# First output product of a two-layer encoder: two block products in other PSUM banks, a residual behind its difference, a scaling ahead of two casts

## The chip, the cores and the metric

The kernel runs on one core of a Trainium2 chip, as one launch. Its five engines are named as in the profile: PE (TensorE, matrix products; PEld is its loading of weights), DVE (VectorE), ACT (ScalarE), POOL (GpSimd) and SP (SyncE, which here only sends transfers; POOL and ACT send some too). Each engine works through its own list in order and waits on semaphores that the others raise. Matrix products write to PSUM, eight banks of 128 x 512 floats. The metric is the time of an execution in microseconds (us), smaller is better.

## The reference, cut to what matters

The input `x` is 512 x 1024 in float32, and there are two layers. `proj` of a layer goes into its token mixer (dilated window attention in layer 0, grouped-query attention in layer 1), into the queries of an attention over 256 memory tokens, and into a gate. The results are gated and go through one output projection, whose product is added to `x`.

```python
for i in range(DEPTH):                       # 2 layers
    h = rmsnorm(x, norm_g[i])
    proj = jnp.einsum('bsd,de->bse', h, w_in_a[j])      # w_in_b in layer 1
    o_mix = mixer_dilated(qkv, ...)          # 8 heads; mixer_axial_gqa in layer 1
    o_mem = memory_attention(q_mem, mem_h, ...)         # 4 heads
    y = jnp.concatenate([o_mix, o_mem], axis=-1) * jax.nn.silu(gate)
    x = x + jnp.einsum('bse,ed->bsd', y, w_out[i])
```

The change lies around the last line of layer 0, "the first output product": `y` is 512 x 1536, `w_out` is 1536 x 1024. The result is both the residual of layer 1 and, normed, the operand of layer 1's projection. Ahead of it stands the end of the eighth window head, where the unnormalized probabilities `p` of its dilations are scaled by softmax weights and added up.

## The kernel before, in words

**Products.** Each float32 product is made in three passes on numbers with fewer bits: high part by high part (line L177), high part by low part of the operand (L178), and low part of the weights by high part of the operand (L181). Weights come from DRAM in pieces of 128 x 1024 (`wl`); ACT casts the high part `wh` (L321), DVE subtracts it for the low part `wo` (L331). One piece serves one step of 12 matmuls: 8 with `wh` (4 on L177, 4 on L178) and 4 with `wo`.

**Seven products for eight.** A chunk is cut into quarters, and `s_chunk` makes it with seven block products in place of eight, from sums of quarters of the operand and of the weights. In the first output product their order is 11, S3, 12, S1, S2, S4, 22 (`PRODUCTS_3`); S2 goes on in the banks of S3, S4 in those of S1. Each has three steps. A product fills two PSUM banks (`bank[s]`, two units of 128 rows), which `s_chunk` takes from the pool `pj` of four banks (`fresh` products only). The other four banks are the pool `at`, from which the attention takes scores, transposes (`pt`, `xT`) and outputs (`oo`). The operand sums are `yS` and their low parts.

**After a product.** A table (`after`) says what follows: `hold` copies the banks to SBUF on ACT (L429: 11, S3 and S1); `add_11` copies 12's banks on ACT (L438) and adds them by DMA (L440); `fold`, after S2, makes on DVE the quarter "21" (`t3`, L447), the quarter "12" and the difference `t5 - t3` (L450), where `t5` is the copy of S1, later the quarter "22"; two `add` at the end finish "12" and "21" on DVE (L422) out of S4 and 22. The difference "22" needs nothing more. The tiles of the four quarters are the halves of the rows' accumulators `acc`.

**The residual.** `ahead` (in `out_proj`) brings `x` in: for quarter "12" by a plain load from SP (L1103), for "21" and "22" by a DMA from POOL that adds into the tile (L1105), for "11" by one too (L1094). The one for "22" is sent right behind the copy of S1 in `hold`, so that DVE's difference (L450) is made out of a tile into which a transfer writes, and waits for it. The one for "21" is sent behind the difference, which reads `t3`.

**Behind it.** When both halves of a block of rows are done, `ev_o` stores them (L1590), takes the sum of squares and norms them on DVE into `m` (L567), PE transposes `m` (`xT`, L573), and the next projection begins (`act`).

**The order.** Nothing is scheduled by a planner: the order of all engines is that in which the program writes the instructions. A `Driver` counts slots, one a step of a product. `release` and `spawn` give it generators that go on when their slot has come, `soon` puts a function at the very start of the next slot, `late` at its end. The eighth head (`attn_a` with `h == 7`) is such a generator; its `scale(1)`, `scale(0)` (L1507 on ACT for this head, four pieces each), `turn` (transposes, L1523, and their copies, L1527) and `pv` (`oo`) are apart by the slots of `Y`. In the slot of `scale(0)` ACT also has a cast of `yS` (L932) and a tanh of the gate (L899).

Of the kernel before, what the change touches and what calls it, by code (L numbers as in the profile page):

```python
# [132 lines left out]
def trunk_kernel(ctx: ExitStack, tc: tile.TileContext, x, mem, wall, norm_g, mem_norm_g, gcol,  # L133
# [9 lines left out]
    drv = Driver()  # L143
# [10 lines left out]
    def pj(name="pj"):  # L154
        return psum.tile([128, 512], F32, tag="pj", name=name, bufs=4)

    def at(name="at"):
        return psum.tile([128, 512], F32, tag="at", name=name, bufs=4)
# [16 lines left out]
    def mm_early(o, a, b, c, d, start):  # L175

        T.matmul(o, a, b, start=start, stop=False, skip_group_check=True)  # L177
        T.matmul(o, c, d, start=False, stop=False, skip_group_check=True)  # L178

    def mm_late(o, a, b, stop):  # L180
        T.matmul(o, a, b, start=False, stop=stop, skip_group_check=True)  # L181
# [208 lines left out]
    def s_chunk(n, act, ev, tokens=True, pre=None, half=False, soon=False, tight=False, place=None, pairs=False, K=4, tail=None, turn=None, late=None, ahead=None):  # L390


        units, per = n // 256, 1024 // n
        bank, snap = [None, None], {}
# [32 lines left out]
        def hold(name, u, b):  # L427
            t = snap[name, u] = place({"z": "11", "s3": "21", "s5": "22"}[name], u)
            A.copy(t, b)  # L429
            if name == "z":  # L430
                ahead("12", u, place("12", u))
            yield 1
            if name == "s5":
                ahead("22", u, t)

        def add_11(name, u, b):
            t = s2(name="sn")
# [6 lines left out]
        def fold(name, u, b):  # L444
            t, t3, t5 = place("12", u), snap["s3", u], snap["s5", u]
            snap[name, u] = t
            V.tensor_tensor(t3, t3, b, ALU.add)  # L447
            V.tensor_tensor(t, t, b, ALU.subtract)
            yield 1
            V.tensor_tensor(t5, t5, t3, ALU.subtract)  # L450
            ahead("21", u, t3)
            yield 1
            yield from ev("22", u, t5)

# [2 lines left out]
        if late is not None:  # L457
            order, runs = PRODUCTS_3, 3
            after = (hold, "z"), (hold, "s3"), (add_11, "z"), (hold, "s5"), (fold, "s2"), (add, "12", "s2"), (add, "21", "s3")
        for i, (a, s, fresh) in enumerate(order):  # L460
            while a not in act:
                drv.tick()
            if fresh:
                bank[s] = [pj() for _ in range(units)]
            for x in range(runs):
                far = late is not None and x == 2
                while far and a not in late:
                    drv.tick()
                wh, wo = [t.rearrange("p (c k e) -> p k c e", c=2, e=256) if pairs else t.rearrange("p (k c) -> p k c", c=n) for t in W.take()]
                ah, al = [(late if far else act)[a][:, v] for v in range(2)]  # L470
                def regions():
                    for b in range(2):
                        o = bank[s][b] if units == 2 else bank[s][0][:, b * 256:(b + 1) * 256]
                        for k in range(per):
                            yield b, k, k if far else x * per + k, slice(b * 128, (b + 1) * 128), o

                if tail and i > 4:
                    if i == 5:
                        drv.free()
                    for b in range(2):  # L480
                        o, ts = bank[s][b], slice(b * 128, (b + 1) * 128)
                        for k in range(per):
                            mm_early(o, ah[:, k, ts], wh[:, k], al[:, k, ts], wh[:, k], False)
                        for k in range(per):
                            mm_late(o, ah[:, k, ts], wo[:, k], k == per - 1)
                        tail[i - 4](b, snap["s5", b], o)
                        drv.free()
                        if i == 5 and b:
                            W.advance()
                        drv.tick()  # L490
                    continue
                for b, k, kk, bs, o in regions():
                    if half and b and k == per // 2:
                        n_half[0] += 1
                        if n_half[0] % half == 0:
                            drv.half()
                    st = fresh and x == k == 0 and (units == 2 or b == 0)
                    if tokens:
                        mm_early(o, ah[:, kk, bs], wh[:, k], al[:, kk, bs], wh[:, k], st)
                    else:  # L500
                        mm_early(o, wh[:, k, bs], ah[:, kk], wh[:, k, bs], al[:, kk], st)
                for b, k, kk, bs, o in regions():
                    if tokens:
                        mm_late(o, ah[:, kk, bs], wo[:, k], x == runs - 1 and k == per - 1)
                    else:
                        mm_late(o, wo[:, k, bs], ah[:, kk], x == runs - 1 and k == per - 1)
                drv.free()
                W.advance()
                if x == runs - 1:
                    f, *arg = after[i]  # L510
                    for u in range(units):
                        d = 2 if f in (keep, hold, fold) or late is not None or tight and i == 1 else 2 + u + (units == 1 and i == 6 and not soon)
                        drv.release(f(*arg, u, bank[s][u]), d)
                drv.tick()
# [329 lines left out]
    def gates(od, o_done, o_here, direct, fused=False, turn=None):  # L844
# [3 lines left out]
        def gate(H, first, g, half=False):  # L848
# [11 lines left out]
            def ev(q, u, t):  # L860
# [56 lines left out]
                ys[2 * j + i] = t  # L917

            s_chunk(256, H, ev, tokens=False, half=half, soon=g == 2, turn=turn)

        def prep_y():
# [150 lines left out]
    def out_proj(YW, ys, src, evac, tiles, half=False, last=None):  # L1072
# [34 lines left out]
        if not last:  # L1107
            s_chunk(512, YW, ev_all, half=half, tight=True, place=place, late=YL, ahead=ahead)
            return
        drv.spawn(prep_l())  # L1110
        s_chunk(512, YW, ev, half=half, tight=True, place=place)

        def ev_l(q, u, t):
# [144 lines left out]
    def place_m(b, j, act=True, p=None):  # L1258

        cs = slice(b * 128, (b + 1) * 128)  # L1260
        split(M.block(0, j, cs), M.block(1, j, cs), p or turn4(mg[b, j], None, None), act)
# [18 lines left out]
    def ahead(u, b):  # L1280

        if (u, b) == (0, 0):
            place_m(1, 0)
            W.hi(True)
            W.hi(True)
        if (u, b) == (0, 1):
            place_m(0, 1)
            place_m(1, 1)
# [114 lines left out]
    def attn_a(h, qk0, qs, ks, v12, n_done):  # L1403
# [98 lines left out]
        def scale(o):  # L1502
            for b in range(4):
                c0, c1 = (64 if o == 0 and b == 0 else 0), (192 if o == 0 and b == 3 else 256)
                pb = prob[o][:, b, c0:c1]
                if h == 7:
                    A.activation(pb, pb, AF.Copy, scale=c[:, o, b:b + 1])  # L1507
                else:
                    V.tensor_scalar(pb, pb, c[:, o, b:b + 1], 0.5, ALU.mult, ALU.mult)

        def turn(o):

            if o:
                parts = [[(b, 0) for b in range(4)]]
                pts[o] = m4(name="pT").rearrange("p (k t) -> p k t", k=2)
                drv.late(lambda: V.transpose(pts[1][:, 1].rearrange("p (b q) -> p b q", b=4), prob[1][:, :, 128:256]))
            else:
                parts = [[(0, 0), (3, 1), (0, 1), (1, 0)], [(1, 1), (2, 0), (2, 1), (3, 0)]]
                pts[o] = [m4(F32R, "pT") for _ in range(2)]
            for i, part in enumerate(parts):  # L1520
                pt = at("pt")
                for n, (b, k) in enumerate(part):
                    T.transpose(pt[:, n * 128:(n + 1) * 128], prob[o][:, b, k * 128:(k + 1) * 128], ident)  # L1523

                def copy(pt=pt, i=i):
                    if o:
                        A.copy(pts[o][:, 0], pt)  # L1527
                    else:
                        js = slice(i * 512, (i + 1) * 512)
                        split(pts[0][0][:, js], pts[0][1][:, js], pt)  # L1530
                drv.late(copy)
# [26 lines left out]
            drv.late(comb)  # L1558

        scale(1)  # L1560
        yield Y[6]
        scale(0)
        turn(1)
        yield Y[7]
        turn(0)
# [9 lines left out]
    for c in A_ORDER:  # L1575
        if c.isdigit():
            drv.later(attn_a(int(c), *head_chunk(int(c))))
        else:
            if c == A_ORDER[-1]:
                drv.spawn(prep_y(), PREP_Y)  # L1580
                drv.spawn(ys[0](), PREP_Y)
            gate(H, *{"m": (8, 0), "a": (0, 1), "b": (4, 2)}[c])
# [338 lines left out]
```

## Time and profile before

| | us |
|---|---|
| three runs | 943.7, 945.46, 948.17 (median 945.46) |
| the profiled execution: its own time | 944.09 |
| its span | 942.3 |
| PE busy in the span | 927.7 (98%) |
| DVE busy | 800.8 (85%) |
| ACT busy | 695.5 (74%) |
| POOL busy | 355.3 (38%) |

The span runs from the first to the last instruction that the trace holds; the execution's own time is 1.8 us longer. Times of single instructions are counted from the span's start. The granted clock of TensorE is 0.999 over the span. The first output product stands between about 566 and 631 us, the end of the eighth head just ahead of it and among its first steps, and layer 1 begins behind it.

The views that are quoted read so. A row of waits: what waited, for which engine and line, how many us in all, how many times, the longest. A row of a timeline: start, length, engine, line, instruction and its tiles, how many in the group, and in brackets the idle time of the engine ahead of it and what ended that. Groups that overlap in time are pipelined: the distance between two starts is what a step takes, not the length of a group. "issue" stands for a wait for which the profile has no name.

### The profile page before, as it was taken

The numbers are of one execution on the slowest core, as the hardware profiler recorded it, in microseconds if no ns is written. First come the engines' busy times: TensorE is split into PE (matmuls) and PEld (weight loads), VectorE is DVE, ScalarE is ACT, GpSimd is POOL, SyncE is SP. The second block draws the span as 40 slices with busy tenths as digits, with TensorE's granted clock in tenths as the row PEclk, the third lists the DMA queues.
The fourth block names the chain that finished last, engine by engine and source line by source line (L and its number), as shares of the span: only waits on it lengthen the run. The fifth ranks groups of instructions, "written<-read, shape, count | busy, mean of one in ns | idle before, by whom it ended". The sixth has DMA issues, their size and how long they took to land.

```text
span 942.3 us, 16240 instructions
## 1 busy us (share of the span) xinstructions
PE 927.7 (98%) x5456; PEld 814.0 (86%) x5456; DVE 800.8 (85%) x1444; ACT 695.5 (74%) x1726; POOL 355.3 (38%) x502
## 2 busy tenths in 40 slices
PE   8999999999999999999999999989999999999998
PEld 6889888888888888888899998778888999998886
DVE  6898677879888888888898989878898998779977
ACT  7775788777768686868686776647878887778774
POOL 3411425455645545454725112216262440111122
PEclk9999999999999999999999999999999999999999
DMA  9999948968777777786868999999985686776777
GB/s 355 387 265 330 283 124 221 313 159 235 183 232 176 233 173 237 163 263 137 269 154 221 257 281 278 301 279 323 273 201 121 168 241 169 198 198 144 183 179 179
DMA packets 84141, 213.97 MB, mean 227 GB/s; under 512 B 19033, under 2 KB 26713, under 8 KB 84058
## 3 DMA queue, kind: packets, MB, share of 16 engines
q1 hardware_dynamic: 61578, 142.21, 41.9%
q0 software_dynamic: 20384, 67.12, 38.6%
q10 hardware_dynamic: 2096, 3.61, 1.0%
q8 instruction: 43, 0.70, 0.3%
q14 instruction: 40, 0.33, 0.1%
HBM read 163.55 MB, written 13.17 MB: 188 GB/s over the span
## 4 chain that ended last, share of the span: by engine, by line
PE 88%; DVE 5%; ACT 4%; issue 1%; DMA 1%; POOL 0%; SPq 0%; DVEq 0%; ACTq 0%; POOLq 0%
PE pj L177 23%; PE pj L178 23%; PE pj L181 23%; PE qT L688 3%; DVE wo L331 2%; PE sa L1435 2%; PE oo L1544 2%; PE ptb L1750 1%; PE sa L1431 1%; PE pt L1523 1%; PE xT L573 1%; ACT wh L321 1%; PE ob L181 1%; PE ob L178 1%; PE ob L177 1%
## 5 line engine op out<-in xcount | busy, mean ns | idle before, releaser
L331 DVE TENSOR_TENSOR wo<-wl,wh 128x1024 fp32r<-128x1024 f32 x261 | 319.8, 1230 | 6.1 <-ACT wh L321 6.0
L321 ACT CAST wh<-wl 128x1024 fp32r<-128x1024 f32 x261 | 275.3, 1060 | 33.7 <-PE pj L178 21.1
L177 PE MATMUL pj<-wh,hS 128*128 128x512 f32 (+1 forms) x416 | 154.3, 380 | 1.5 <-ACT kmT L725 1.5
L178 PE MATMUL pj<-wh,hS 128*128 128x512 f32 (+1 forms) x416 | 149.1, 367 | 0.1
L177 PE MATMUL pj<-wh,h 128*128 128x512 f32 (+1 forms) x312 | 115.2, 378 | 0.0
L178 PE MATMUL pj<-wh,h 128*128 128x512 f32 (+1 forms) x312 | 111.6, 367 | 0.0
L521 POOL TENSOR_TENSOR rstd<-mse,half 128x4 f32<-128x4 f32 (+2 forms) x98 | 100.9, 1030 | 8.2
L181 PE MATMUL pj<-wo,hS 128*128 128x512 f32 (+1 forms) x416 | 99.5, 366 | 0.0
L177 PEld LDWEIGHTS pj<-wh,hS 128*128 128x128 f32 x416 | 78.6, 189 | 12.6 <-ACT kmT L725 1.7
L178 PEld LDWEIGHTS pj<-wh,hS 128*128 128x128 f32 x416 | 78.7, 189 | 11.6 <-DVE hS L652 0.3
L520 POOL TENSOR_SCALAR mse<-hss 128x4 f32<-128x4 f32 (+1 forms) x88 | 47.1, 535 | 110.2 <-ACT junk L676 102.6
L181 PEld LDWEIGHTS pj<-wo,hS 128*128 128x128 f32 x416 | 72.5, 189 | 13.1
L676 ACT ACTIVATE junk<-sn 128x128 f32<-128x128 f32 x264 | 79.3, 311 | 1.7 <-DVE sn L412 1.7
L259 POOL DMA_DIRECT2D wl<-in_wall_dram x44 | 41.6, 967 | 100.8 <-ACT pb L1734 21.8
L1376 POOL TENSOR_TENSOR ta<-sn,tabs 128x128 f32<-128x128 f32 (+1 forms) x64 | 37.2, 587 | 111.4 <-DVE sn L681 87.3
L399 ACT COPY sn<-pj 128x512 f32<-128x512 f32 x122 | 67.2, 590 | 12.5 <-PE pj L181 12.5
L181 PE MATMUL pj<-wo,h 128*128 128x512 f32 (+1 forms) x312 | 74.5, 365 | 0.0
L305 POOL DMA_DIRECT2D wl<-wl x35 | 31.0, 895 | 99.2 <-DVE wo L331 44.0
L422 DVE TENSOR_TENSOR sn<-pj,sn 128x512 f32<-128x512 f32 x89 | 60.7, 682 | 7.1 <-PE pj L181 6.7
L178 PEld LDWEIGHTS pj<-wh,h 128*128 128x128 f32 x312 | 59.0, 189 | 8.3
L177 PEld LDWEIGHTS pj<-wh,h 128*128 128x128 f32 x312 | 59.0, 189 | 8.2
L295 POOL DMA_DIRECT2D wl<-wl x35 | 32.9, 974 | 80.5 <-DVE wl L290 18.7
(293 smaller groups left out, 2377.6 us busy)
## 6 DMA issues: line engine op xcount, KB each, us to landing
wl<-in_wall_dram SPq DMA_DIRECT2D x226, 512.0 KB, 8.4
wl<-wl POOLq DMA_DIRECT2D x70, 512.0 KB, 5.8
wl<-in_wall_dram POOLq DMA_DIRECT2D x48, 512.0 KB, 8.2
od<-o SPq DMA_DIRECT2D x11, 256.0 KB, 3.8
x<-in_x_dram SPq DMA_DIRECT2D x4, 512.0 KB, 8.9
v0r<-sn SPq DMA_DIRECT2D x8, 256.0 KB, 10.5
v0d<-v0r SPq DMA_DIRECT2D x4, 512.0 KB
og<-od ACTq DMA_DIRECT2D x4, 512.0 KB, 11.1
```

The lines of the kernel that those rows point to most:

```text
L177: T.matmul(o, a, b, start=start, stop=False, skip_group_check=True)
L178: T.matmul(o, c, d, start=False, stop=False, skip_group_check=True)
L181: T.matmul(o, a, b, start=False, stop=stop, skip_group_check=True)
L259: queue.dma_start(t, wall[d], **how)
L321: A.copy(wh, self.tile[self.items[i]])
L331: V.tensor_tensor(wo, self.tile[key], wh.bitcast(F32), ALU.subtract)
L399: A.copy(t_, b_)
L422: V.tensor_tensor(t_, b_, t_, ALU.subtract if q == "12" and late is None else ALU.add)
L520: G.tensor_scalar(e, ss, EPS, None, ALU.add)
L521: G.tensor_tensor(r, e, half[:, 0:n], ALU.pow)
L676: A.activation(jk, p[:, j * 128:(j + 1) * 128], AF.Square, scale=by, accum_out=ss[:, j:j + 1])
L1376: G.tensor_tensor(ta[:, 0:n], xn[:, 0:n, 0:32], ropeA[:, 0, b, s0:s0 + n], ALU.mult)
```

## The change

Three edits, all at the first output product:

1. the second (S3) and the fourth (S1) of the seven products take their banks from the pool `at`; S2 and S4, which go on in them, follow. The other three products stay in `pj`;
2. the add of `x` into quarter "22" is sent in `fold`, behind the difference and behind the add for "21", and no longer in `hold`;
3. in the eighth head `scale(0)` stands at the very start of the next slot, ahead of the cast and the tanh of that slot.

```diff
@@ hold
             yield 1
-            if name == "s5":
-                ahead("22", u, t)
@@ fold
             V.tensor_tensor(t5, t5, t3, ALU.subtract)
             ahead("21", u, t3)
+            ahead("22", u, t5)
             yield 1
@@ s_chunk
             if fresh:
-                bank[s] = [pj() for _ in range(units)]
+                bank[s] = [at("pj") if late is not None and i in (1, 3) else pj() for _ in range(units)]
@@ attn_a
         scale(1)
+        if h == 7:
+            drv.soon(lambda: scale(0))
         yield Y[6]
-        scale(0)
+        if h < 7:
+            scale(0)
         turn(1)
```

`late is not None` holds for this product alone. No engine has an instruction more or less. What the rows below call by a number at a name is one tile; lines of the changed kernel are lower by one or two behind the first edit. `DMASW` counts are landings of transfers that POOL sent, `DMAHW` of those of SP and ACT.

ACT at the end of the eighth head, before:

```order
L321 CAST wh<-wl 128x1024
L1507 ACTIVATE p<-p,c 128x256 x4
L399 COPY sn<-pj 128x512
L321 CAST wh<-wl 128x1024
L932 CAST yS_7119<-ys 128x512 x2
L899 ACTIVATE th<-sn 128x512
L1507 ACTIVATE p<-p,c 128x192
L1507 ACTIVATE p<-p,c 128x256 x2
L1507 ACTIVATE p<-p,c 128x192
```

and now:

```order
L321 CAST wh<-wl 128x1024
L1506 ACTIVATE p<-p,c 128x256 x4
L399 COPY sn<-pj 128x512
L321 CAST wh<-wl 128x1024
L1506 ACTIVATE p<-p,c 128x192
L1506 ACTIVATE p<-p,c 128x256 x2
L1506 ACTIVATE p<-p,c 128x192
L931 CAST yS_7123<-ys 128x512 x2
L898 ACTIVATE th<-sn 128x512
```

The four scalings of `scale(0)` have passed the two casts of `yS` and the tanh; the first four are `scale(1)`.

PE where product 12 (`yl12`) ends and S1 (`yS1`) begins, before:

```order
L181 MATMUL pj_7328<-wo_7320,yl12_7356 128x512 x2
L181 MATMUL pj_7329<-wo_7320,yl12_7356 128x512 x2
L177 MATMUL pj_7407<-wh_7348,yS1_7351 128x512 [waits Activation_49]
L178 MATMUL pj_7407<-wh_7348,yS1_7351 128x512
L177 MATMUL pj_7407<-wh_7348,yS1_7351 128x512
```

and now:

```order
L181 MATMUL pj_7328<-wo_7320,yl12_7356 128x512 x2
L181 MATMUL pj_7329<-wo_7320,yl12_7356 128x512 x2
L177 MATMUL pj_7407<-wh_7348,yS1_7351 128x512 [waits PE_49]
L178 MATMUL pj_7407<-wh_7348,yS1_7351 128x512
L177 MATMUL pj_7407<-wh_7348,yS1_7351 128x512
```

The order is the same, the first matmul of S1 waits for a count of PE itself in place of one of ACT.

DVE from the difference on (`acc` is the difference's tile, `m` the normed rows that PE transposes), before:

```order
L331 TENSOR_TENSOR wo_7568<-wl_6880,wh_7567 128x1024 [waits DMASW3_49,Activation_49]
L450 TENSOR_TENSOR acc_7342<-acc_7342 128x512 [waits DMASW2_49,DVE_49]
L450 TENSOR_TENSOR acc_7343<-acc_7343 128x512 [waits DMASW3_49,DVE_49]
L331 TENSOR_TENSOR wo_7586<-wl_6942,wh_7585 128x1024 [waits DMASW4_49,PE_49,Activation_49]
L567 SCALAR_TENSOR_TENSOR m_7524<-m_7524,rm_73,row_7522 128x512 [waits DMAHW2_49,DMAHW1_49]
```

and now:

```order
L331 TENSOR_TENSOR wo_7566<-wl_6880,wh_7565 128x1024 [waits DMASW3_49,Activation_49]
L448 TENSOR_TENSOR acc_7342<-acc_7342 128x512 [waits DVE_49]
L448 TENSOR_TENSOR acc_7343<-acc_7343 128x512 [waits DVE_49]
L331 TENSOR_TENSOR wo_7584<-wl_6942,wh_7583 128x1024 [waits DMASW4_49,PE_49,Activation_49]
L566 SCALAR_TENSOR_TENSOR m_7524<-m_7524,rm_73,row_7522 128x512 [waits DMAHW2_49,DMAHW1_49]
```

The waits of the two differences for a transfer of POOL are gone; nothing else on DVE has moved. On POOL the six adds of `x` before were sent in the order 11, 11, 22, 22, 21, 21, and now in 11, 11, 21, 22, 21, 22.

## The prediction, on record before the run

> **What bounds the kernel now.** I read the page first, then TensorE's waits in the stretch of the first output product, then its timeline there, and last what the engines that feed it do at the same places. The page:
>
> ```profile
> span 942.3 us, 16240 instructions
> PE 927.7 (98%) x5456; PEld 814.0 (86%) x5456; DVE 800.8 (85%) x1444; ACT 695.5 (74%) x1726; POOL 355.3 (38%) x502
> ```
>
> TensorE (PE) is busy for 98% of the span. Its order of work is fixed, so time that it waits in the middle is time of the whole, as long as nobody else is late afterwards. Its waits from 555 to 655 us (what waited, for whom; us, times, longest), then two stretches (length; busy us of PE, PEld, DVE, ACT, POOL; clock, DMA share, GB/s):
>
> ```profile
> PE xT L573 <- issue: 2.3, 1, 2.3
> PE pj L177 <- ACT sn L438: 1.5, 1, 1.5
> PE pt L1523 <- ACT p L1507: 0.8, 1, 0.8
> PE pj L177 <- ACT acc L429: 0.2, 1, 0.2
> ```
>
> ```profile
> 560.00:570.00 10.00, 9.19 (x58) 7.91 (x57) 10.00 (x15) 9.68 (x19) 2.59 (x3) 1.00 0.99 265
> 620.00:630.00 10.00, 7.58 (x42) 5.96 (x41) 9.30 (x13) 4.29 (x9) 1.34 (x2) 1.00 0.82 202
> ```
>
> Four waits, 4.8 us in all, and the edits aim at each of them: the scaling at the 0.8, the banks at the 0.2 and the 1.5, the residual at the 2.3. What a wait really costs is read from the starts of the groups (start, length, instruction, count, idle before):
>
> ```profile
> 564.36 0.27 PE L1523 MATMUL pt<-ident,p 128*128 128x128 f32 x1
> 565.44 0.96 PE L1523 MATMUL pt<-ident,p 128*128 128x128 f32 x7 [0.81 <-ACT p L1507]
> 566.15 0.47 PE L177 MATMUL pj<-wh,y 128*128 128x512 f32 x1
> ...
> 574.94 0.40 PE L177 MATMUL pj<-wh,yS 128*128 128x512 f32 x1
> ...
> 580.41 0.39 PE L177 MATMUL pj<-wh,ylS 128*128 128x512 f32 x1
> ...
> 583.51 0.50 PE L177 MATMUL pj<-wh,y 128*128 128x512 f32 x1 [0.22 <-ACT acc L429]
> ...
> 589.11 0.39 PE L177 MATMUL pj<-wh,yl 128*128 128x512 f32 x1
> ...
> 593.46 0.50 PE L177 MATMUL pj<-wh,yS 128*128 128x512 f32 x1 [1.47 <-ACT sn L438]
> ...
> 615.35 0.39 PE L177 MATMUL pj<-wh,ylS 128*128 128x512 f32 x1
> ...
> 618.07 0.39 PE L177 MATMUL pj<-wh,y 128*128 128x512 f32 x1
> ...
> 623.28 1.34 PE L573 MATMUL xT<-ident,m 128*128 128x128 f32 x8 [2.33 <-issue]
> 624.38 0.48 PE L177 MATMUL pj<-wh,y 128*128 128x512 f32 x1
> ...
> 627.20 1.08 PE L573 MATMUL xT<-ident,m 128*128 128x128 f32 x8
> 628.03 0.48 PE L177 MATMUL pj<-wh,yl 128*128 128x512 f32 x1
> ```
>
> One step of a product (12 matmuls, 0.227 us from one to the next) goes from start to start in 2.72 us where nothing waits (615.35 to 618.07), eight transposes in 0.83 (627.20 to 628.03).
>
> **The scaling moved ahead.** No instruction is added. On ACT the four scalings of `p` now stand before the cast of `yS` and the tanh:
>
> ```profile
> 562.14 1.14 ACT L932 CAST yS<-ys 128x512 fp32r<-128x512 f32 x2
> 563.72 1.58 ACT L1507 ACTIVATE p<-p,c 128x192 f32<-128x192 f32 x4
> ```
>
> They then end at 562.14 + 1.58 = 563.72, before 564.36, and the eight transposes take 0.83 instead of 566.15 - 564.36 = 1.79: term 1 is 0.96 us. The price is paid by what is passed: `yS` and the tanh start 1.58 later. `yS` is first multiplied at 574.94; its cast ends at about 564.9 instead of 563.3, and its low half on VectorE (DVE) behind it by some 0.5 us later, with 9 us to spare. DVE is the engine to fear, busy 10.00 of 10.00 us there, but its own lead over PE (below) covers half a microsecond.
>
> **The banks.** S3 and S1 now accumulate in the pool of the transposes. In both places the wait on ACT that names the bank's copy is gone; in its place PE waits for a count of its own, of the products with `p` of the last heads, which stand ahead of 574.94 in its order and are long past. ACT's copies do not disappear, they only stop holding PE:
>
> ```profile
> 584.79 1.15 ACT L932 CAST yS<-yf 128x512 fp32r<-128x512 f32 x2
> ```
>
> From 580.41 to 583.51 is 3.10, less 2.72: term 2 is 0.38. From 589.11 to 593.46 is 4.35, less 2.72: term 3 is 1.63. What is late next at S1 is its operand, cast from 584.79 to 585.94, while PE comes at about 593.46 - 2.97 = 590.5: nothing waits. The other tenants of the pool are the transposes of `m` at 623 and 627 us. They take S3's banks, copied out at 584, and then those of S1 and S4, which L422 reads ahead of the second `m`; no new wait.
>
> **The residual behind the difference.** DVE no longer waits for the add by DMA before L450; the add is issued by GpSimd behind it, each right after that of the quarter "21":
>
> ```profile
> 612.05 2.35 DVE L331 TENSOR_TENSOR wo<-wl,wh 128x1024 fp32r<-128x1024 f32 x2
> 618.43 0.69 DVE L450 TENSOR_TENSOR acc<-acc 128x512 f32<-128x512 f32 x1 [4.03 <-DMA acc<-in_x_dram]
> 620.70 0.69 DVE L450 TENSOR_TENSOR acc<-acc 128x512 f32<-128x512 f32 x1 [1.57 <-DMA acc<-in_x_dram]
> 622.44 1.41 DVE L567 SCALAR_TENSOR_TENSOR m<-m,rm,row 128x512 f32<-128x512 f32 x2
> ...
> 632.09 1.28 DVE L422 TENSOR_TENSOR acc<-pj,acc 128x512 f32<-128x512 f32 x2
> ...
> 637.07 3.48 DVE L331 TENSOR_TENSOR wo<-wl,wh 128x1024 fp32r<-128x1024 f32 x3
> ```
>
> The unnamed 2.33 us of PE's xT is this: `m` is normed at 622.44, behind both waits. Without the stall the first transpose would start at 618.07 + 2.72 = 620.79 and the step behind it at 621.62 instead of 624.38: term 4 is 2.76. DVE must keep up. Even if it came no sooner to 612.05, its two L450 (0.69 each), one wo (2.35 / 2) and the norm (1.41) end at 614.40 + 1.4 + 1.2 + 1.4 = 618.4, the first half of `m` at 617.7; PE, 2.97 us ahead by then, comes at 617.8. That is level, at worst some 0.3 us of wait if `m` is a little later than that; the saved DVE time is 4.03 + 1.57 = 5.60, about what PE gains, so DVE's lead in the stretch behind keeps its size.
>
> **The sum** is 0.96 + 0.38 + 1.63 + 2.76 = 5.73 us. The waits alone give 0.81 + 0.22 + 1.47 + 2.33 = 4.83, the lower bound where each step behind a stall keeps its slow start. The profiled execution took 944.09 us (span 942.3), the median of the three runs is 945.46, so it ran a little under the median; 942.3 - 5.7 is a span of 936.6, the profiled execution 938.4, and the median 945.46 - 5.73 = 939.7.
>
> **What the moved adds cost.** GpSimd's timeline, and the landings of all four adds of line L1105 (min, median, max):
>
> ```profile
> 607.93 2.15 POOL L1105 DMA_DIRECT2D acc<-in_x_dram  x2
> 619.61 0.86 POOL L1105 DMA_DIRECT2D acc<-in_x_dram  x1 [9.53 <-DVE acc L450]
> 621.75 0.86 POOL L1105 DMA_DIRECT2D acc<-in_x_dram  x1 [1.27 <-DVE acc L450]
> ```
>
> ```profile
> DMA to landing us min/median/max: 4.0/7.3/12.1
> ```
>
> The longest are the "22" pair: what DVE waited for until 620.70 was sent at about 608.5. The pair of "21", sent at 619.61 and 621.75, has the shortest. Now four of them leave between 615 and 618, the second "21" as third, at about 616.9. L422 wants it, for its second half, at 632.09 + 0.64 = 632.73 less 5.73, 627.0. At 4.2 us it lands at 621.1, with 5.9 to spare; at 12.1 at 629.0, and DVE is held 2.0 us. I take a value nearer the first, since the stretch from 620 is the one with 0.82 of DMA share and 202 GB/s. Nothing hides such a hold: of the three low weights (wo) of 637.07 the first ends at 637.07 + 3.48 / 3 = 638.23, and PE takes it up with the third of these four matmuls,
>
> ```profile
> 638.14 1.07 PE L181 MATMUL pj<-wo,act 128*128 128x512 f32 x4
> ```
>
> at 638.14 + 2 x 0.227 = 638.59. The lead is 0.36. The "22" adds are wanted only by the norm behind L422.
>
> [...]
>
> **The rivals.**
> *Late residual.* As worked out: landing in 12.1 us, DVE held 2.0, PE 2.0 less the 0.36 of lead = 1.6. Gain 4.1, time 941.4. For it: 10.4 to 12.1 at 608. Against it: 4.0 to 4.2 at 620.
> *Given back.* PE is early, but DVE, full at 10.00 of 10.00 us, or the weight loads are not, and PE waits later for what it saved; between half of it and all comes back, time 942.6 to 945.5. For it: the DMA share of 0.99 and DVE's load. Against it: the first of the two wo of 612.05 ends at 613.2 and is taken up by PE at 615.35 + 8 x 0.227 = 617.2, so DVE has some 4 us in hand there, and the largest of PE's waits from 640 us to the end name no weight and no DMA:
>
> ```profile
> PE pj L177 <- ACT kmT L725: 1.5, 1, 1.5
> PE pmt L815 <- DVE pmT L821: 0.7, 1, 0.7
> ```
>
> *Slower.* The same late residual at its worst: one weight load (L259) sent between 570 and 576 us needed
>
> ```profile
> DMA to landing us min/median/max: 16.4/16.4/16.4
> ```
>
> An add sent at 616.9 would then land at 633.3, behind the 632.73 of today, and DVE is 0.6, PE 0.6 - 0.36 = 0.2 us later than now: 945.7. It decides from a landing of 632.73 + 0.36 - 616.9 = 16.2 us; only below that is there a gain.
> *Not what it says.* If the pool's next bank were one still being read, S1 would wait there again: 5.73 - 1.63 - 0.38 = 3.7, time 941.7. The order names only transposes and products already ended, so I hold this small.
>
> **How the numbers follow.** Four stalls gone: 0.63, 939.7, with a range of its own from 937.5 to 941.5 (the waits alone at 940.6, and the run-to-run spread of the median of runs from 943.7 to 948.17). Late residual 0.15; given back 0.13; slower 0.06; not what it says 0.03. The range for 8 in 10 is 936.0 to 944.4: it takes in the late residual, most of what is given back, and below the forecast the 1.76 us by which the lowest of the three runs lay under their median, doubled. A measurement tells about 0.5% from no change, 4.7 us. The forecast lies only 1 us beyond that, so about four fifths of its 0.63 and a third of the late residual's 0.15 are faster: 0.55. Slower by over 4.7 us has no mechanism of that size; 0.05 for what I don't see. The rest, 0.40, is no difference.
>
> **What would show it.** In the profile after: the eight transposes near 564 unbroken; steps of 2.72 us at S1 and at the third product; L450 twice without idle time; xT of `m` at about 617.8 with less than 0.3 us of wait. Wrong it is if xT still waits over 1 us, if L422 near 626 waits for a DMA, if a wo near 632 ends behind its use, or if PE has a new wait of over 1 us behind 640 us.

## The result, and the profile after

The changed kernel takes 938.43 us (median of five runs, 937.85 to 940.67) against 946.25 before (median of five, 943.7 to 948.17). The ratio is 0.9921, with a 95% interval from 0.9898 to 0.9944: 7.5 us less, between 5.3 and 9.7. The two profiled executions took 944.09 and 938.43, 5.66 us apart.

Two things in the part ahead of the prediction are wrong. S2 goes on in the banks of product 11, not in those of S3 (in `PRODUCTS_3` both have the number 1 for `bank[s]`), so with the change only S4 follows into the pool `at`. And `m` does not hold rows of `x`: it is the memory tokens' rows, normed for layer 1 (`mem_norm`), which come from DRAM and have nothing to do with the residual. That `m` waited for the residual's transfers was a matter of DVE's order alone; an experiment below tests it.

The page after, and PE's waits over the whole span (what waited, for whom; us, times, longest):

```profile
span 936.7 us, 16239 instructions
PE 927.0 (99%) x5456; PEld 814.7 (87%) x5456; DVE 800.8 (85%) x1444; ACT 695.3 (74%) x1726; POOL 353.0 (38%) x502
```

```profile
PE row L1233 <- DMA row<-in_mem_norm_g_dram: 2.3, 1, 2.3
PE pj L177 <- ACT kmT L724: 1.7, 1, 1.7
PE pmt L814 <- DVE pmT L820: 0.7, 1, 0.7
```

These are the longest three. All four waits of the stretch are gone from the list; what is left lies at the start of the span or behind 655 us. PE's timeline at the same places as before:

```profile
564.53 1.03 PE L1522 MATMUL pt<-ident,p 128*128 128x128 f32 x8
565.32 0.48 PE L177 MATMUL pj<-wh,y 128*128 128x512 f32 x1
...
579.55 0.39 PE L177 MATMUL pj<-wh,ylS 128*128 128x512 f32 x1
...
582.27 0.39 PE L177 MATMUL pj<-wh,y 128*128 128x512 f32 x1
...
587.71 0.39 PE L177 MATMUL pj<-wh,yl 128*128 128x512 f32 x1
...
590.55 0.39 PE L177 MATMUL pj<-wh,yS 128*128 128x512 f32 x1
...
615.03 0.39 PE L177 MATMUL pj<-wh,y 128*128 128x512 f32 x1
...
617.75 1.03 PE L572 MATMUL xT<-ident,m 128*128 128x128 f32 x8
618.54 0.48 PE L177 MATMUL pj<-wh,y 128*128 128x512 f32 x1
```

The distances (from the starts before rounding) are now 0.79 (transposes of `p`), 2.72 (S3 to 12), 2.83 (12 to S1), 2.73 and 0.79 (22 to `m`, and `m`'s transposes). DVE's and POOL's rows that answer to those before, and the landings of the four adds (min, median, max):

```profile
612.44 1.28 DVE L448 TENSOR_TENSOR acc<-acc 128x512 f32<-128x512 f32 x2
...
614.78 1.40 DVE L566 SCALAR_TENSOR_TENSOR m<-m,rm,row 128x512 f32<-128x512 f32 x2
...
624.96 1.28 DVE L422 TENSOR_TENSOR acc<-pj,acc 128x512 f32<-128x512 f32 x2
```

```profile
613.75 3.57 POOL L1104 DMA_DIRECT2D acc<-in_x_dram  x4 [5.10 <-DVE acc L448]
```

```profile
DMA to landing us min/median/max: 6.5/8.6/10.7
```

The two differences run without a wait, the norm of `m` starts at 614.78, 3 us ahead of PE's transposes. The adds landed in 6.5 to 10.7 us, between the 4 and the 12 of before, and L422 did not wait for them.

### The profile page after: what moved, and what is told of

Same layout as the page of the kernel before. It is cut to its first block, busy times and chain, and to the rows that moved or that the text cites. A ratio compares the mean times of both kernels' runs of the same rounds, so it can differ in the third digit from the quotient of the medians.

```text
span 936.7 us, 16239 instructions
## 1 busy us (share of the span) xinstructions
PE 927.0 (99%) x5456; PEld 814.7 (87%) x5456; DVE 800.8 (85%) x1444; ACT 695.3 (74%) x1726; POOL 353.0 (38%) x502
## 3 DMA queue, kind: packets, MB, share of 16 engines
q10 hardware_dynamic: 2096, 3.61, 1.0%
## 4 chain that ended last, share of the span: by engine, by line
PE 90%; DVE 4%; ACT 2%; DMA 2%; issue 1%; POOL 0%; DVEq 0%; SPq 0%; ACTq 0%; POOLq 0%
PE pj L177 24%; PE pj L178 24%; PE pj L181 24%; PE qT L687 3%; DMA wl<-in_wall_dram 2%; PE sa L1434 2%; PE oo L1543 2%; PE ptb L1752 1%; PE sa L1430 1%; DVE wo L331 1%; PE pt L1522 1%; PE xT L572 1%; PE ob L181 1%; PE ob L178 1%; PE ob L177 1%; PE sb L172 1%
## 5 line engine op out<-in xcount | busy, mean ns | idle before, releaser
L399 ACT COPY sn<-pj 128x512 f32<-128x512 f32 x122 | 67.2, 590 | 12.6 <-PE pj L181 12.5
L422 DVE TENSOR_TENSOR sn<-pj,sn 128x512 f32<-128x512 f32 x89 | 60.7, 683 | 7.1 <-PE pj L181 6.7
```

The lines of the kernel that those rows point to most:

```text
L399: A.copy(t_, b_)
L422: V.tensor_tensor(t_, b_, t_, ALU.subtract if q == "12" and late is None else ALU.add)
```

## The experiments

Executions differ by a few microseconds in where the first output product starts (561 to 565 us). So the table goes by distances between starts on PE, from the profiled execution of each kernel: (a) from the first matmul of product 11 to the one behind the eight transposes of `p`; (b) the third step of S3, up to product 12; (c) the third step of 12, up to S1; (d) the first step of 22, up to `m`'s first transpose; (e) from there to the transposes of its second block; and the stretch from the first matmul of 11 to the first transposes of `acc`. Beside it the median of all runs and how many had a mean granted clock below 0.999 (the kernel before: 16 of 29, 21 of 35 and 18 of 26 in the three groups of experiments, with medians of 946.26, 946.2 and 947.21). Kernels of different groups are compared by their ratios to before; their medians can differ by about 1 us for this alone.

| kernel | a | b | c | d | e | stretch | median us | low clock |
|---|---|---|---|---|---|---|---|---|
| before | 4.62 | 3.11 | 4.35 | 5.22 | 3.92 | 77.52 | 946.25 | |
| changed | 3.63 | 2.72 | 2.83 | 2.73 | 3.61 | 71.45 | 938.43 | 0 of 5 |
| banks + scaling | 3.63 | 2.72 | 3.56 | 7.98 | 6.42 | 80.23 | 948.3 | 12 of 12 |
| residual | 5.20 | 3.11 | 4.35 | 2.73 | 3.62 | 75.25 | 943.29 | 0 of 12 |
| residual + banks | 4.54 | 2.72 | 2.72 | 2.73 | 3.61 | 72.25 | 940.09 | 0 of 6 |
| residual + scaling | 3.63 | 3.16 | 5.21 | 2.73 | 3.62 | 74.60 | 941.81 | 3 of 12 |
| banks | 5.20 | 2.72 | 2.72 | 7.70 | 5.71 | 80.00 | 946.2 | 12 of 12 |
| scaling | 3.63 | 3.16 | 5.04 | 6.55 | 6.45 | 81.11 | 946.43 | 10 of 12 |
| banks + scaling, filled | 3.64 | 2.72 | 3.69 | 8.44 | 4.53 | 78.96 | 945.27 | 1 of 12 |
| before, filled | 4.64 | 3.10 | 4.36 | 5.08 | 3.96 | 77.43 | 944.46 | 0 of 12 |
| `m` early | 5.22 | 3.10 | 4.36 | 2.73 | 5.18 | 77.11 | 945.91 | 4 of 12 |
| 11 early + banks + scaling | 5.21 | 2.72 | 2.77 | 5.26 | 5.50 | 77.40 | 941.72 | 5 of 12 |
| adds swapped | 3.65 | 2.72 | 3.71 | 2.73 | 3.62 | 72.56 | 940.57 | 3 of 7 |
| add to 11 early | 3.63 | 2.72 | 3.56 | 2.73 | 3.61 | 72.18 | 940.3 | 0 of 6 |

Just ahead of column (a) PE can wait for the first four scalings (0 to 1.5 us), and this shows in (a): where a lower clock follows, (a) grows by 1.6 us (`m` early, with a clock of 0.66 from 565 to 570 us; 11 early has the same 1.6), and where the next four scalings are late too, by waits of 0.3 and 0.8 (residual, banks). Kernels with the same order of work here differ in it (5.20 in "residual", 4.62 before), so these differences are not put down to an edit. Executions differ by 2 to 3 us even at full clock, so the medians of two kernels tell less than the columns.

The theory formed from the two traces is "one clock" (not TensorE's clock is meant, but the time that somebody else sets): PE's wait for `m` ends when the adds for 22 have landed, whatever PE does ahead of it. Its rival is the prediction's own "sum", where each term stands by itself.

**Without the residual's edit.** The changed kernel with the add of 22 put back:

```diff
+            if name == "s5":
+                ahead("22", u, t)
...
-            ahead("22", u, t5)
```

> The banks and the scaling as changed, the residual left where it was. Theory 'one clock' (formed from the two traces): the first transpose of m follows the DMA adds of the quarter 22, and these are sent by POOL behind the adds for 11, which wait for the transfers acc<-sn; those landed at 604.41 and 607.05 us before and at 604.84 and 607.44 after, though PE was 3 us ahead by then. So PE comes 2.97 us earlier and waits 2.97 us longer: xT of m still starts at 623.3 (+-0.5), its wait grows from 2.33 to about 5.3, and the time is that of before within 0.5 us. Theory 'sum' (the terms of the prediction stand each by itself): 2.97 us faster, xT at 620.3 with a wait of 2.3.

Measured: 948.3 against 946.26, ratio 1.0015 (0.9997 to 1.0034); no gain at all, so "sum" falls. The edits (a), (b) and (c) did their work, 2.5 us less on the way to 22 (54.07 in place of 56.54 us from the start of the stretch, counting a wait of 0.8 that is new in c), and the wait for `m` took it all: `m`'s first transpose starts 62.0 us into the stretch, before 61.8. POOL's timeline, PE's, and PE's clock by windows (length; busy us of PE, PEld, DVE, ACT, POOL; clock, DMA share, GB/s):

```profile
606.30 0.87 POOL L1094 DMA_DIRECT2D acc<-in_x_dram  x1 [9.80 <-DMA acc<-sn]
608.96 0.87 POOL L1094 DMA_DIRECT2D acc<-in_x_dram  x1 [1.80 <-DMA acc<-sn]
609.52 2.13 POOL L1105 DMA_DIRECT2D acc<-in_x_dram  x2
```

```profile
624.60 1.97 PE L573 MATMUL xT<-ident,m 128*128 128x128 f32 x8 [5.09 <-DVE m L567]
...
627.23 0.63 PE L177 MATMUL pj<-wh,y 128*128 128x512 f32 x1
```

```profile
615.00:620.00 5.00, 4.51 (x20) 3.39 (x19) 0.59 (x1) 1.05 (x1) 0.00 (x0) 1.00 1.08 305
620.00:625.00 5.00, 0.40 (x2) 0.40 (x3) 3.04 (x5) 0.00 (x0) 1.72 (x2) 0.86 0.78 172
625.00:630.00 5.00, 5.00 (x17) 4.24 (x16) 5.00 (x9) 2.12 (x3) 0.00 (x0) 0.50 0.92 266
630.00:635.00 5.00, 5.00 (x26) 4.21 (x26) 3.93 (x6) 3.35 (x10) 0.87 (x2) 0.96 1.01 374
```

The adds of 22 leave right behind those of 11, and these behind transfers that POOL waits for (9.80 and 1.80 us). And then something that neither theory had: behind the wait of 5.09 us PE works at half its clock. A matmul takes 0.63 in place of 0.39, the step behind the transposes 4.79 in place of 2.83; (e) is 6.42 in place of 3.92. With the 0.3 by which `m` comes later, this makes the stretch 2.7 us longer than before.

**The residual alone, with the banks, with the scaling.** The kernel before with the `hold` and `fold` lines of the change; with these and the `bank` line; with these and the `attn_a` lines.

> Only the residual moved; banks and scaling as before. Both theories: the waits of 0.8, 0.2 and 1.5 us stay, xT of m starts at 618.07 + 2.72 = 620.8 in place of 623.28 and the step behind it 2.76 us earlier; time 2.8 us under before. Theory 'one clock' adds that this edit is the one without which the others are worth nothing, 'sum' that it is worth 2.76 of 5.73. A third theory, that DVE is the bound (prediction: level at 618), would show a wait of xT over 0.3 us.

> Residual and banks, scaling as before. Both theories: with the residual out of the way the terms add: 2.76 + 2.01 = 4.8 us under before, that is 0.9 to 1.0 over the changed kernel; the transposes near 564 us wait 0.8 again. If DVE bounds m, part of the 1 us of the scaling is not there and the time is that of the changed kernel.

> Residual and scaling, banks as before. Both theories: 2.76 + 0.96 = 3.7 us under before; the waits of the third product (0.2) and of S1 (1.5 on ACT's copy of product 12) are back. If S1's wait is really one for its operand and not for the bank, the wait of 1.5 is there in the changed kernel in another place, and this kernel is as fast as the changed one.

Measured: ratios 0.996 (0.9942 to 0.9979), 0.9934 (0.991 to 0.9958) and 0.9952 (0.9934 to 0.9971). In all three (d) is 2.73, with no wait of `m`, so DVE is not the bound there. From 22 to the step behind the transposes of `m` the residual is worth 2.79 us (5.22 + 1.09 less 2.73 + 0.79), as forecast. The banks on top of it are worth 75.25 - 72.25 = 3.0 of the stretch and the scaling 75.25 - 74.60 = 0.65, where 2.0 and 1.0 were expected. For the banks, columns (b) and (c) give 3.11 + 4.35 less 2 x 2.72, that is 2.02, as expected; 0.66 of the rest is column (a), which is no effect of them. For the scaling, (a) gives 1.57 (0.99 against before's 4.62), and (b) and (c) take 0.91 back. The reason stands in PE's waits of residual + scaling:

```profile
PE pj L177 <- ACT sn L436: 2.1, 1, 2.1
PE pj L177 <- ACT acc L429: 0.3, 1, 0.3
```

PE arrives 1 us earlier at S1, whose banks ACT frees when it does: 1.5 has become 2.1, 0.2 has become 0.3. So without the banks the scaling is nearly swallowed at the next waits, and banks that come on top of the scaling are credited with it: the expected 2.0 over the changed kernel for the banks left out is 3.1 of the stretch (74.60 - 71.45) and about 2.9 by the ratios (0.9952 and 0.9921).

**Banks alone, scaling alone.**

> Only the banks. 'Sum': 2.0 us faster than before. 'One clock': xT of m starts when it did (61.8 us behind the first step of the product), so PE's wait there grows from 2.3 to 4.3 us and nothing is gained by it. With what the run of banks and scaling showed (a wait of 5.1 us, the clock at 0.50 from 625 to 630 and 2.7 us lost), 'one clock' has a second part: whether the clock falls after 4.3 us tells where the bound lies; if it falls, 2 to 2.8 us slower than before's profiled execution, if not, the same.

> Only the scaling. 'Sum': 1.0 us faster. 'One clock': the waits behind it take it up: S1 still starts 31.9 us behind the first step, since its wait ends with ACT's copy of product 12 (1.5 grows to some 2.3), xT still at 61.8, nothing gained; the clock stays at 1.00 in the stretch as long as the wait of xT is no longer than the 2.33 of before.

Measured: 946.2 and 946.43 against 946.2, ratios 0.9996 (0.9979 to 1.0014) and 1.0005 (0.9987 to 1.0023). Neither is worth anything without the residual's edit. `m`'s transposes start 62.5 and 62.9 us into the stretch; the waits there grew to

```profile
PE xT L573 <- DVE m L567: 4.8, 1, 4.8
```

with the banks and to

```profile
PE xT L573 <- issue: 3.7, 1, 3.7
```

with the scaling, longer than expected (4.3, and the 2.33 of before), and behind both the clock fell, to 0.50 from 625 to 630 us. With the scaling:

```profile
620.00:625.00 5.00, 1.33 (x7) 0.90 (x6) 3.18 (x5) 0.00 (x0) 1.72 (x2) 0.85 0.58 115
625.00:630.00 5.00, 5.00 (x17) 4.12 (x16) 5.00 (x8) 2.11 (x3) 0.00 (x0) 0.50 0.97 268
```

**Is it the clock? The wait filled with idle work.** Two kernels, banks + scaling with 48 and the one before with 20 of

```diff
+            if layer and b == 0:
+                warm = at("warm")
+                for k in range(48):
+                    T.transpose(warm[:, k % 4 * 128:(k % 4 + 1) * 128], ident, ident)
             for j in range(2):
                 norm_3(t[b], M, b * 128, j)
```

> Banks and scaling without the residual, as in the run that was slower than before, but PE does 48 transposes of the identity into a spare bank (48 x 0.1 = 4.8 us) while it waits for m; nothing reads them. If the loss there is the clock, which falls while PE does nothing: the clock stays at 1.00 behind the wait, the eight transposes take 0.8 and the step behind them 2.8 in place of 1.6 and 4.8, and the time is 2.7 us below that run, that is before's. If the loss is something else that a late m brings (weights, DVE), it stays.

> The kernel before with 20 transposes of the identity (2.0 us) in the wait of 2.33 us ahead of m; nothing reads them. Of the runs of before listed beside the experiments 15 of 29 have a mean clock of 0.999 or 1.000 and 943.0 to 945.6 us (one of them 948.0), the others 0.996 to 0.998 and 945.9 to 951.3. If the same clock makes these, it falls behind this wait in about half of the executions, and with the wait filled nearly all runs have 0.999 or 1.000 and the median is 944.5, some 1.7 under before. If the clock falls somewhere else, the runs fall in two groups as before.

Measured: banks + scaling falls from 948.3 to 945.27 (against 946.2, ratio 0.9993, 0.9975 to 1.0011), with one run of 12 under 0.999 in place of 12. The clock of the profiled execution, for the same windows as above:

```profile
620.00:625.00 5.00, 5.00 (x44) 4.79 (x43) 1.77 (x3) 0.00 (x0) 0.89 (x2) 1.00 0.98 264
625.00:630.00 5.00, 4.08 (x27) 3.30 (x26) 5.00 (x8) 2.12 (x3) 0.83 (x1) 1.00 0.80 192
```

The step behind the transposes takes 2.86. The transposes themselves still take 1.7, now because of two waits in them (0.3 for `m`, 0.6 for DVE's L422, which the bank of the idle transposes brought in); so that part of what was expected did not come, and the stretch is only 1.3 us shorter than unfilled (78.96 against 80.23). The step behind them, where most of the loss was, is back to its length at full clock. The kernel before, filled, has no run of 12 under 0.999, against 21 of 35 unfilled, and a median of 944.46 against 946.2. The ratio is 0.9987 with an interval from 0.9971 to 1.0004, which does not quite exclude an unchanged time; that the low clock is gone stands in the counts. So in more than half of its runs the kernel before loses clock behind the wait of `m`, some 1.9 us by the medians of the runs at 0.999 or more and of those below (944.85 and 946.72; in the two other groups of experiments 4.2 and 4.1 us lie between them, more than the clock alone takes in any trace here), and its profiled execution (clock 0.999, 944.09 us) was one that did not. (The expectation counted 15 of 29 runs at full clock; there are 13.)

**Does `m` need the residual?** The kernel before with `m`'s first block normed one slot earlier, ahead of the differences on DVE:

```diff
-        yield MEM_D
+        yield MEM_D - layer
         norm_2(t[0], rm[:, 0:1], rows["m"])
-        yield 1
+        yield 1 + layer
```

> The kernel before, all three edits undone; only the norming of the first block of m stands one slot earlier on DVE, ahead of the two differences that wait for the DMA adds. m is made of the memory rows and holds nothing of the residual. If its lateness is only its place in DVE's queue: the first transposes of m start without a wait, 2.8 us earlier; the second block, which still stands behind the differences, is normed at 61.8 + 2.3 = 64.1 us behind the first step of the product while PE comes at 62.9 and waits 1.2; from the first step to the transposes of acc 76.0 us in place of 77.5, the clock 0.999 or 1.000 in nearly all runs, the median 943 (1.5 below the 944.5 of the filled run). If m needs the adds, nothing changes.

Measured: 945.91 against 947.21, ratio 0.9979 (0.9959 to 0.9999). PE's timeline:

```profile
624.88 1.03 PE L573 MATMUL xT<-ident,m 128*128 128x128 f32 x8
...
630.06 1.34 PE L573 MATMUL xT<-ident,m 128*128 128x128 f32 x8 [1.41 <-issue]
```

The first block comes without a wait, the second, still behind the differences, with one of 1.41 (1.2 expected). So it was DVE's order, no need. The rest did not come as said: the stretch is 77.11, not 76.0. 0.6 of that is column (a) (5.22 in place of 4.62): PE waited 1.5 us for the first scalings just ahead of it, and the clock then fell (0.66 from 565 to 570 us). The other 0.5 is missing behind: from the start of S1 the stretch is 1.0 shorter than before (44.61 in place of 45.59), not 1.5. The 8 runs at 0.999 or more have a median of 943.5; 4 of 12 lie below, where nearly none was expected.

**Is POOL's queue what made the adds late?** Banks + scaling, with the add of 11 sent behind the copy of 11:

```diff
             if name == "z":
                 ahead("12", u, place("12", u))
+                ahead("11", u, t)
...
             if q == "11":
-                G.dma_start(t, src[b][:, n * 512:(n + 1) * 512], accum_op=ALU.add)
                 yield 2
```

> Banks and scaling; the residual of quarter 22 stays in its old place, but that of quarter 11 is added right behind the copy of product 11 (before the sum with product 12 and not after it), so that POOL has no add left that waits for a transfer. If the adds of 22 were late because POOL's queue was held by those of 11 (9.2 and 1.8 us of waiting), they now leave at 603 to 604, right behind ACT's copies of S1, land within 10 to 12 us by 616, the differences wait at most 1 us and PE's wait for m falls from 5.1 to under 1: 71.5 to 73 us from the first step to the transposes of acc, time 938.5 to 940. If it is the landing alone, or ACT, the wait stays over 3.

Measured: 941.72 against 947.21, ratio 0.9947 (0.9926 to 0.9968), where banks + scaling had 1.0015. POOL's and PE's rows, and PE's clock:

```profile
607.07 1.80 POOL L1105 DMA_DIRECT2D acc<-in_x_dram  x2 [3.73 <-ACT acc L429]
```

```profile
624.98 1.32 PE L574 MATMUL xT<-ident,m 128*128 128x128 f32 x8 [2.38 <-DVE m L568]
...
627.56 0.63 PE L177 MATMUL pj<-wh,y 128*128 128x512 f32 x1
```

```profile
625.00:630.00 5.00, 4.99 (x18) 3.92 (x19) 5.00 (x8) 2.12 (x3) 0.00 (x0) 0.66 1.11 286
```

The adds now wait for ACT's copy alone and leave 42.2 us into the stretch in place of 47.0. But they land in 12.6 and 14.7 us in place of 9.8 and 11.9, so of 4.7 us only 1.9 arrive. POOL's queue was one cause, the slower landing the other (the DMA share does not tell the two apart: 1.08 from 615 to 620 us in both); the wait is 2.38 where less than 1 was expected, and even this one was followed by a slow clock. The two adds of 11 that now leave at 579 us, and the sums with product 12 that leave later than they did (601 us, 595 in banks + scaling), are a possible reason for the slow landing, which was not tried by itself. This profiled execution was the slowest of the 12 (947.18 us), with 1.6 us lost in (a) as well; the 7 runs at 0.999 or more have a median of 941.07, and how long their wait is the record does not show.

**The add that DVE wants first, sent last.** The changed kernel with the two `ahead` lines of `fold` exchanged:

> The changed kernel with the adds of 21 and 22 in the other order, so that the add that DVE wants first (21 of the second unit) is the last of four. In the changed kernel they landed at 620.24, 622.24, 624.25 and 626.24 (6.5 to 10.7 us), and DVE comes to the second half of L422 at 625.6. So DVE is held some 0.6 us, of which PE, whose tightest low weight had 1.2 us to spare, sees nothing: time as the changed kernel within 0.3 us. The rival 'late residual' of the prediction says that every us of such a hold beyond that lead costs one; here it would cost 0.6 if the lead is not there.

Measured: 940.57 (7 runs), ratio 0.9934 (0.9906 to 0.9963). DVE's timeline:

```profile
627.93 0.68 DVE L422 TENSOR_TENSOR acc<-pj,acc 128x512 f32<-128x512 f32 x1
630.09 0.69 DVE L422 TENSOR_TENSOR acc<-pj,acc 128x512 f32<-128x512 f32 x1 [1.47 <-DMA acc<-in_x_dram]
...
634.48 3.49 DVE L331 TENSOR_TENSOR wo<-wl,wh 128x1024 fp32r<-128x1024 f32 x3
```

The hold is 1.47, not 0.6, since the fourth add landed 11.5 us behind its sending, and PE lost 0.21 in the step that takes these low weights. That is near the rule by which the prediction priced the rival, the hold less the lead (1.47 less 1.2 in the changed kernel). Behind it PE's wait for `kmT` grew from 1.7 to 2.2, and the clock fell:

```profile
660.00:665.00 5.00, 2.77 (x24) 2.56 (x24) 5.00 (x8) 4.17 (x7) 0.45 (x1) 1.00 1.09 206
665.00:670.00 5.00, 5.00 (x30) 5.00 (x31) 4.38 (x5) 2.94 (x11) 1.88 (x2) 0.66 1.05 279
```

So the order 21 before 22 is worth 0.21 us in this trace, and the bunch of adds stands nearer the edge than the changed kernel's trace shows. Whether the hold made the wait for `kmT` longer was not tried, and the ratios of the two kernels (0.9934 and 0.9921) don't tell them apart.

**What is left behind the stretch.** The changed kernel with DVE's add of product 11 (`sn`, L422) ahead of other work in the 256-wide chunk at 660 us:

```diff
+                        if early and i == 1:
+                            g = f(*arg, u, bank[s][u])
+                            drv.soon(lambda g=g: drv.urgent.append([drv.slot + max(1, next(g)), g]))
+                        else:
-                        drv.release(f(*arg, u, bank[s][u]), d)
+                            drv.release(f(*arg, u, bank[s][u]), d)
```

> The changed kernel with one more edit behind the stretch: in the first 256-wide chunk of layer 1 DVE's add that frees the banks of product 11 (L422) stands ahead of other work in its slot. PE waits 1.66 us there for an instruction of ACT by the profile, while DVE's add ends at 661.01 and PE starts at 661.16. If DVE's add is what ends the wait, PE starts 0.5 to 1.2 us earlier and the time falls by as much; if it is ACT, nothing changes.

Measured: 940.3 (6 runs), ratio 0.9928 (0.9903 to 0.9952), no better than the changed kernel. The wait named after ACT was DVE's: from the transposes of `acc` to that step PE is 1.6 us quicker (26.4 in place of 28.0). PE's waits behind 655 us:

```profile
PE pj L177 <- DVE sn L422: 0.8, 1, 0.8
PE pmt L818 <- DVE pmT L824: 0.8, 1, 0.8
PE pj L178 <- DVE hS L655: 0.4, 1, 0.4
PE pj L177 <- ACT hS L654: 0.4, 1, 0.4
```

The three of 0.8, 0.4 and 0.4 on `pj` are new, on the same two engines, and take all of it back: by 695 us the kernel is 0.65 us behind the changed one, counted from the transposes of `acc`. An earlier place for one of DVE's instructions made others late.

## Why the prediction was right, and where it was not

The time (939.7 predicted, 938.43 measured) and the likeliest case, four stalls gone, came out; for the profiled execution 938.4 was predicted and 938.43 measured. By the terms, from the two traces:

- **Scaling:** 0.96 predicted; the eight transposes went from 1.79 to 0.79, 1.00.
- **Banks at product 12:** 0.38 predicted, 3.11 to 2.72, 0.39.
- **Banks at S1:** 1.63 predicted, 4.35 to 2.83, 1.52. "What is late next" was not `yS`, as the prediction had it, but the low part of product 12's last operand (`yl`, DVE), a step earlier: 0.1 us in this execution, 0.8 to 1.0 in four others with the scaling and the banks (column c).
- **Residual:** 2.76 predicted, 5.22 + 1.09 to 2.73 + 0.79, 2.79; `m`'s first transpose at 617.75, predicted 617.8.
- **Sum:** 5.70 against 5.73. The steps behind the stalls at 583.51 and 593.46 us start slowly (2.88 and 2.85 us, where the changed kernel has 2.72 for both), which gives 0.3 of the 0.4 more (the whole stretch is 6.07 shorter); 0.2 went back at the wait for `kmT`, and the execution entered the stretch 0.2 later. The span is 5.6 shorter.

The *late residual* did not come about: the landings of 6.5 to 10.7 us lay well above the value taken (near 4.2), but the third of them, the one that L422 needs, came at 624.25 against a need at 625.6. The margin was 1.3 us where the prediction had 5.9, so that nothing was lost there is partly luck. The value near 4.2 was taken because 620 to 630 us had a DMA share of 0.82; but that share belonged to the stall. From 620 to 625 us it is 0.70 with PE waiting and 1.09 in the changed kernel, where PE works on. The lead was mis-sized too: in the changed kernel the first of the three low weights is ready 1.2 us ahead of its use, where the prediction had 0.36. The last two adds (9.3 and 10.7 us) came nearer to the rival's 12.1 than to 4.2, the first two (6.5 and 8.0) did not. Exchanging two of the adds made the landing cost 0.21 us of PE. DVE was no bound either: the prediction had `m` level with PE at 617.7, and its norm started at 614.78. *Given back* came to 0.2 us. *Not what it says* did not come about, the waits for the banks are gone.

Two steps were wrong in kind, though the sum hides it. First, the terms were worked out as if each edit had its price. Two of the three have none by themselves: banks, scaling and both together are worth nothing without the residual's edit, because the wait for `m` ends when POOL's transfers have landed (`m`'s first transpose starts 62.5, 62.9 and 62.0 us into the stretch, 61.8 before). The 5.7 us are a price of all three. Second, the sum was set against the median of the runs (945.46 - 5.73), though it was made on an execution at full clock. By the medians the gain is 7.8; about 1.7 of it is probably what the filled kernel showed (946.2 less 944.46), the half clock behind the wait for `m` in over half of the runs of before, which the profiled execution doesn't have. The prediction's working has no such term. It came within 1.3 us of the median all the same, since three runs gave 945.46 and five 946.25; that the missing term was small against the range is luck.

## What to carry to other kernels

A stall on the engine that bounds the kernel ends when something else is done. If that does not itself depend on how far the engine has come, work saved ahead of the stall is worth nothing until the stall is gone (ratios of 0.9996, 1.0005 and 1.0015 here): remove the stall furthest downstream first, and price edits together, in the order of the path.

A wait of a few microseconds on PE can cost more than itself: in six profiled executions the clock fell behind one, which took 1.7 or 3.4 us more. For a wait that can't be removed, idle transposes are worth a try: they kept the clock up in 23 of 24 runs here (1.7 us by the medians of the kernel before, with an interval that just includes no gain), and the granted clock of single runs tells whether it is needed even when the profiled execution looks clean.

An engine's queue can make dependences that the data do not have: normed one slot earlier on DVE, `m`'s first block came without the wait of 2.33 us. Ask of a late instruction what stands ahead of it on its engine before asking what it reads.

## What the runs showed of the hardware that was not expected

**The clock.** In six profiled executions PE's clock fell behind a wait ahead of the kernel's end, which cost one of two amounts of time. Where a whole window of 5 us lies in the fall it reads 0.50, and matmuls that start 0.23 us apart otherwise start 0.43 apart (627.23 and 627.65 us with banks + scaling). Added over the windows, the loss is 1.7 us behind waits of 1.5 (`m` early), 2.38 (11 early) and 2.2 (adds swapped): each has one window of 5 us at 0.66, which lacks 0.34 x 5 = 1.7. Behind waits of 3.7 (scaling), 4.8 (banks) and 5.1 (banks + scaling) it is 3.4 us, for the last one 0.14 x 5 + 0.50 x 5 + 0.04 x 5, part of it during the wait: from 620 to 625 us 0.7 us are lost, and PE starts again only at 624.60. Behind 2.33 us in the profiled execution of before it was nothing (1.00 from 620 to 630 us). Behind the wait of 2.38 the fall comes late: the eight transposes took 1.08 us, as behind the 2.33 of before (1.10), and the matmuls are 0.43 apart only from 626.71 us on.

So the length of a wait alone does not decide. Waits of 1.5 and 2.2 us had a fall behind them, and the 2.33 of before had none, nor is one to be seen for the 2.1 of residual + scaling, whose mean clock is 1.000. Of the 90 runs of before in the three groups 55 had the low clock, some of them perhaps for another wait. What else decides, these runs do not show.

**Adds by DMA.** The four adds of the changed kernel were sent within 1.8 us and landed 2.0 us apart (6.5, 8.0, 9.3 and 10.7 us behind their sending); the same 256 KB took 4.0 to 4.2 before, where two were sent 2.1 us apart. Not only the bunch differs: the first of the four took 6.5 already, at a DMA share of 1.08 from 615 to 620 us, where before it was 0.70 from 620 to 625. So the price taken beside the stall (4.0 to 4.2 us) did not hold where the stall was gone.
